# Attention with side work for the next four heads: 1.7 side steps per key block in place of 1.3

## The chip, the cores and the metric

The kernel runs on one core of one Trainium2 chip. The metric is the device time of one execution in microseconds; of the kernel before three executions are at hand, and their median is the time before. A profiled execution, recorded by the hardware, gives the trace from which all durations here are read.

## The reference

One inference step of a small decoder with two layers, for a prompt of 1024 tokens (16 learned meta tokens ahead of it) and for 8 samples of 4 new tokens that share the weights. The first layer is a causal convolution module and a feed-forward block with a convolution, the second is multi-head latent attention and the same kind of feed-forward block. The change is in the prompt's attention, which the reference computes so (cut; queries and keys are first normalised per head, and the last 32 values of a query are rotated by its position):

```python
def rms_norm(x, g):
    xf = x.astype(jnp.float32)
    y = xf * lax.rsqrt(jnp.mean(xf * xf, axis=-1, keepdims=True) + NORM_EPS)
    return (y * g.astype(jnp.float32)).astype(x.dtype)

def mla_queries(xn, pos, w_dq, q_lat_norm, w_uq, qnorm_nope, qnorm_rope):
    q = jnp.einsum('btl,lhd->bthd', rms_norm(xn @ w_dq, q_lat_norm), w_uq)
    q_nope = rms_norm(q[..., :QK_NOPE], qnorm_nope)
    q_rope = rope(rms_norm(q[..., QK_NOPE:], qnorm_rope), pos)
    return q_nope, q_rope
...
    k_nope = rms_norm(jnp.einsum('btc,chd->bthd', c, w_uk), knorm_nope)
    v = jnp.einsum('btc,chd->bthd', c, w_uv)
...
        s = (jnp.einsum('bqhd,bkhd->bhqk', qn_b, k_nope) +
             jnp.einsum('bqhr,bkr->bhqk', qr_b, kr)).astype(jnp.float32) * SM_SCALE
        s = jnp.where(kpos[None, :] <= qpos[:, None], s, NEG)
        p = jax.nn.softmax(s, axis=-1).astype(v.dtype)
        return jnp.einsum('bhqk,bkhd->bqhd', p, v)
```

There are 16 heads with 64 + 32 values per query and key and 64 values per output, in float32. The scores' precision is kept by splitting each operand into a high and a low part and multiplying three times (high by high, high by low, low by high).

## The kernel before, in words

The program goes through the phases one after the other: the first layer, then the prompt's attention (about 1415 to 1830 us in the profile), then the samples and the last feed-forward block. Only the attention's loop is touched.

**The loop.** One head after the other, n = 0 to 15. In head n, `values` takes the two halves of 512 queries: 5 key blocks for the first half and 9 for the second, so 14 blocks, counted x = 0 to 13. A block is three score matmuls of TensorE (L1347, L1349, L1350) into a PSUM tile p, the causal mask added on the diagonal by VectorE (L1352), the exponential by ScalarE into pf (L1354), and then the value matmul of the block before (L1337), so that TensorE has the scores of one block to do while the exponential of the last one runs. The width of a block is the number of queries that may see it: 512 for the early blocks, then 400, 272, 144 and 16 at the end of a half.

**What runs beside it.** At fixed x of head n the program calls steps for head n + 1: `query` (x = 0, transposes L1277 and splits into high and low, L135 to L138), `scores` (at the x in SAT; L1307, with the row maximum on VectorE, L1309 to L1314) and `shift` (x = SHAT = 12), which transposes the maxima (L1319, TensorE) and puts them as a further row into the query tile (L1323, VectorE). The first score matmul of head n + 1 needs L1323. `keys` comes at x = 8 to 10 of every second head, `metas` at x = 7 of every fourth; `finish` normalises a pair of heads on GpSimd's queue (L1380 on VectorE, L1384 on GpSimd).

**The side work.** Queries and keys are projected for four heads at a time, a group. At x = SIDE = 8 of heads 0, 4 and 8 a generator `side` is made for the next group. For groups 2 and 3 it has some 30 steps:
- `group_k`, 10 steps: the load of the weights; 5 steps of two blocks (matmuls L151, copy and square on ScalarE, sums L1160 on VectorE); the reciprocal root (`rsqrt`, L255 to L260, VectorE); three multiplies on GpSimd.
- `group_q`, 20 steps: the load; 9 projection steps, each six matmuls L151 of 384 columns, two copies L1193 and a square L1196 on ScalarE and the sums L1201 on VectorE; the reciprocal root, whose result is the tile rrq; then three pieces of three steps each: a multiply of q by rrq on GpSimd (L1209), a multiply on VectorE (L1215), and the rotation on VectorE (four multiplies L1103, then L1106 and L1107).

For group 1 the side work has 20 steps, since `group_q`'s projections are done before the loop: `group_k` and the scaling and rotary steps alone.

**Its pace.** At the end of every block the loop adds RATE (L46) to `due`, and takes one step of `side` for each whole 1 in it. What is left of `side` is run at x = 0 of the group's last head.

**What sets the final order.** The program is written in this order, and a scheduler then reorders each engine's queue by its own estimate of times and by the free buffers: score tiles p turn over in 3 PSUM buffers, which the projections use too, value tiles in 2, pf in 4.

Of the kernel before, what the change touches and what calls it, by code (L numbers as in the profile page):

```python
# [42 lines left out]
BLOCKS = ((0, 8), (8, 7), (15, 7))  # L43
WQ = 5
LAG = 3
RATE = 1.3  # L46
QAT = 0
AAT = (14, 34)
BAT = (12, 80)
# [69 lines left out]
class Prog:  # L119
# [989 lines left out]
    def attention(self, es):  # L1109
# [302 lines left out]
        def both(g):  # L1412
            yield from group_k(g)
            yield from group_q(g)
# [42 lines left out]
        for n in range(H):  # L1457
# [3 lines left out]
            for x, _ in enumerate(chain(values(n, 0), values(n, 1))):  # L1461
# [18 lines left out]
                if n % 4 == 0 and x == SIDE and n < H - 4:  # L1480
                    side = both(g + 1) if g else chain(group_k(1), nxt)
                due += RATE
                while due >= 1:
# [408 lines left out]
```

## Time and profile before

| | us |
|---|---|
| time, median of 3 executions | 2760.52 (2760.06 to 2764.99) |
| the profiled execution, its own time | 2764.3 |
| its span (first to last instruction) | 2762.4 |
| from head 0's L1319, just ahead of the attention loop, to head 15's | 1415.4 to 1801.4 |

The span is 1.9 us below the profiled execution's own time. TensorE's granted clock is 0.981 of full speed on the mean. In the views, a row has the busy time of an engine, or of a group of instructions (line, engine, operation, tile written from tiles read), with how many there were; a bracket at a row's end is the idle time of the engine ahead of it, and what ended that. PE is TensorE, PEld its weight loads, DVE VectorE, ACT ScalarE, POOL GpSimd, SP SyncE.

### The profile page before, as it was taken

To read this page: it belongs to the slowest core of one execution; us is meant where nothing else is said; L and a number is where in the kernel's file an instruction comes from. 1 tells how busy PE (TensorE), PEld (TensorE's weight loads), DVE (VectorE), ACT (ScalarE), POOL (GpSimd) and SP (SyncE) were. 2 spreads that over 40 slices of the span, in tenths; PEclk is the share of its full clock that TensorE was granted. 3 is DMA by queue.
4 is the path that set the end of the run, shared out by engine and by line. 5 is a ranking of instruction groups with operands and counts; after the bars stand their busy time and mean duration, and the time that the engine had idled before them with its cause. 6 is when DMAs were issued, how large, how long until landed. Compare 5 with 4: busy or idle time off the path is not lost.

```text
span 2762.4 us, 46569 instructions
## 1 busy us (share of the span) xinstructions
PE 2652.8 (96%) x16966; PEld 2448.0 (89%) x16966; DVE 1878.0 (68%) x3485; ACT 1356.2 (49%) x3701; POOL 711.0 (26%) x1019
## 2 busy tenths in 40 slices
PE   7999997999999999999889999999999999999999
PEld 6888876999999999999767776667999999999999
DVE  8899986578888875135677767676377777775232
ACT  6777775345444553023555555566245454453010
POOL 1567663024333330001111212110023333330000
PEclk9999997999999999999989999999999999999999
DMA  4211101502322236123100001267402222227122
GB/s 142 57 41 55 39 29 42 173 32 87 95 88 94 80 105 238 47 81 107 35 11 18 26 24 32 80 199 261 152 24 89 80 77 85 80 97 244 41 87 76
DMA packets 127769, 238.24 MB, mean 86 GB/s; under 512 B 39778, under 2 KB 81140, under 8 KB 127412
## 3 DMA queue, kind: packets, MB, share of 16 engines
q1 hardware_dynamic: 103828, 200.82, 22.6%
q0 software_dynamic: 9600, 32.36, 3.1%
q10 hardware_dynamic: 14112, 2.09, 0.5%
q8 instruction: 133, 2.18, 0.3%
q14 instruction: 96, 0.79, 0.1%
HBM read 183.90 MB, written 51.31 MB: 85 GB/s over the span
## 4 chain that ended last, share of the span: by engine, by line
PE 85%; DVE 6%; ACT 5%; DMA 2%; issue 2%; POOL 0%; SPq 0%; ACTq 0%; DVEq 0%; POOLq 0%
PE ps L796 30%; PE ps L175 22%; PE pk L654 5%; PE v L1337 5%; PE g L419 4%; PE ps L845 3%; PE p L151 2%; PE ps L197 2%; PE ps L1013 1%; PE po L1651 1%; PE p L1347 1%; PE p L1350 1%; PE p L1349 1%; PE s L1307 1%; PE sn L151 1%
## 5 line engine op out<-in xcount | busy, mean ns | idle before, releaser
L135 ACT ACTIVATE wh<-raw 128x512 fp32r<-128x512 f32 (+2 forms) x256 | 191.1, 749 | 542.0 <-PE ps L175 338.5
L136 DVE TENSOR_TENSOR wl<-raw,wh 128x512 fp32r<-128x512 f32 (+2 forms) x244 | 201.5, 829 | 111.4 <-ACT wh L135 109.2
L942 DVE TENSOR_TENSOR x<-ps,x 128x1074 f32<-128x1074 f32 (+1 forms) x48 | 61.0, 1270 | 293.1 <-PE ps L175 293.1
L766 DVE SCALAR_TENSOR_TENSOR c<-ub,c,c 128x1040 f32<-128x1040 f32 (+1 forms) x176 | 225.1, 1312 | 28.6 <-ACT c L763 27.6
L761 POOL COPY sb<-ub 128x32 f32<-128x32 f32 x88 | 88.8, 1011 | 400.9 <-DVE ub L807 363.2
L669 ACT ACTIVATE qq<-pk 128x64 f32<-128x64 f32 x736 | 158.1, 243 | 67.6 <-PE pk L654 67.5
L1337 PE MATMUL v<-pf,vf 128*128 128x512 f32 (+4 forms) x448 | 176.6, 478 | 10.0 <-ACT pf L1354 9.7
L663 POOL TENSOR_TENSOR sq<-sq 128x256 f32<-128x256 f32 (+4 forms) x229 | 140.2, 623 | 102.6 <-ACT sq L658 95.6
L175 PE MATMUL ps<-xh,wh 128*128 128x358 f32 (+1 forms) x672 | 148.3, 329 | 9.1 <-ACT xh L135 5.9
L1354 ACT ACTIVATE pf<-p 128x512 f32<-128x512 f32 (+4 forms) x224 | 99.0, 451 | 118.1 <-DVE p L1352 98.1
L669 ACT ACTIVATION_READ_ACCUMULATOR qq<-pk 128x1 f32 x736 | 153.9, 227 | 0.0
L523 DVE SCALAR_TENSOR_TENSOR a<-u,c,a 128x512 f32<-128x512 f32 x216 | 150.1, 745 | 4.9 <-ACT a L516 4.9
L175 PE MATMUL ps<-xh,wl 128*128 128x358 f32 (+1 forms) x672 | 147.6, 328 | 0.0
L175 PE MATMUL ps<-xl,wh 128*128 128x358 f32 (+1 forms) x672 | 147.4, 327 | 0.1
L175 PE MATMUL ps<-al,wh 128*128 128x358 f32 (+1 forms) x672 | 147.2, 327 | 0.0
L175 PE MATMUL ps<-ah,wl 128*128 128x358 f32 (+1 forms) x672 | 146.5, 326 | 0.0
L175 PE MATMUL ps<-ah,wh 128*128 128x358 f32 (+1 forms) x672 | 146.2, 326 | 0.0
L654 PE MATMUL pk<-ukh,ch 128*128 128x512 f32 x256 | 115.5, 452 | 25.6 <-ACT ch L135 13.4
L763 ACT ACTIVATE c<-ub,c 128x1074 f32<-128x1074 f32 (+1 forms) x88 | 101.3, 1185 | 59.7 <-DVE ub L807 46.8
L175 PEld LDWEIGHTS ps<-xh,wh 128*128 128x128 f32 x672 | 117.5, 191 | 12.7 <-ACT xh L135 6.8
L658 ACT ACTIVATE sq<-pk 128x512 f32<-128x512 f32 x164 | 99.8, 613 | 50.8 <-PE pk L654 48.5
L135 ACT ACTIVATE wh<-s 128x512 fp32r<-128x512 f32 x120 | 75.7, 631 | 94.9 <-PE ps L796 88.3
(599 smaller groups left out, 9100.4 us busy)
## 6 DMA issues: line engine op xcount, KB each, us to landing
raw<-wup SPq DMA_DIRECT2D x88, 512.0 KB, 3.5
pg<-ctn SPq DMA_DIRECT2D x128, 192.0 KB, 3.8
raw<-wdn SPq DMA_DIRECT2D x32, 448.0 KB, 3.3
raw<-pw SPq DMA_DIRECT2D x24, 512.0 KB, 3.9
d_a<-c POOLq DMA_DIRECT2D x22, 537.0 KB, 3.5
raw<-d_a SPq DMA_DIRECT2D x22, 537.0 KB, 5.2
d_a<-c POOLq DMA_DIRECT2D x22, 531.0 KB, 3.1
raw<-d_a SPq DMA_DIRECT2D x22, 531.0 KB, 5.3
```

The lines of the kernel that those rows point to most:

```text
L135: return (nc.scalar.activation(h, src, AF.Copy), (eng or nc.vector).tensor_tensor(out=l, in0=src, in1=h.bitcast(F32), op=ALU.subtract))
L136: (eng or nc.vector).tensor_tensor(out=l, in0=src, in1=h.bitcast(F32), op=ALU.subtract))
L175: nc.tensor.matmul(p[:, c, :ch], s[:, k * 128:(k + 1) * 128], m[k][:, off + c * ch:off + (c + 1) * ch], start=k == 0 and i == 0, stop=k == ...
L419: y = nc.tensor.matmul(p[:, 0], x[:, k * 128:(k + 1) * 128], m[k][:, t * ch:t * ch + ch], start=k == 0 and i == 0, stop=k == KD - 1 and i ...
L523: nc.vector.scalar_tensor_tensor(out=p[:, :ND] if j == n - 1 else acc, in0=x[:, j:j + ND], scalar=w[:, j:j + 1], in1=to if j == 1 else acc ...
L654: x = nc.tensor.matmul(ps, s[:, j, :], m[:, 512 * c:512 * c + 512], start=i == 0, stop=i == 2)
L663: nc.gpsimd.tensor_tensor(out=to, in0=v[:, :, :n], in1=v[:, :, n:2 * n], op=ALU.add)
L669: nc.scalar.activation(q, ps[:, 64 * h:64 * h + 64], AF.Square, accum_out=ss[:, p, 8 * c + h:8 * c + h + 1])
L763: x = nc.scalar.activation(c, ub, AF.Copy, scale=wd[:, t, 2:3])
L766: nc.vector.scalar_tensor_tensor(out=c[:, 2:pe], in0=ub[:, tap:tap + pe - 2], scalar=wd[:, t, tap:tap + 1], in1=c[:, 2:pe], op0=ALU.mult, ...
L796: nc.tensor.matmul(ps, w[:, s], m[:, lo:hi], start=first and k == 0 and i == 0, stop=k == KD // 2 - 1 and i == 2, skip_group_check=True)
L1337: nc.tensor.matmul(o[:, at_:], vf[:m, b, c], p[:m, :512 - at_], start=b == 0, stop=last)
```

## The change

The change is one number: the loop takes 1.7 side steps per block in place of 1.3.

```diff
-RATE = 1.3
+RATE = 1.7
```

The loop that uses it, which is as before:

```python
                due += RATE
                while due >= 1:
                    due -= 1
                    next(side, None)
```

For group 2 (made in head 4 at x = 8) the keys' steps end in head 4 rather than at the start of head 5; the nine projection steps of the queries come in head 5 at x = 0 to 5, before at x = 3 to 9; and the scaling and rotary steps at x = 6 to 11 of head 5, before from x = 10 of head 5 to x = 2 of head 6. Group 3 is the same in heads 8 to 10. For group 1 the scaling and rotary steps come in head 1 at x = 0 to 5, before at x = 2 to 9. No engine gets another instruction, and SyncE's queue is as before. The places that matter follow, in the order that the scheduler gives each engine.

**VectorE, where group 2's q is scaled and rotated.** rrq is the scale, q_... the q tile of group 2, scr scratch; L1352 masks a block's scores p. Before, in head 6:

```order
L1215 TENSOR_TENSOR scr<-q_18839,rrq 128x512
L1312 TENSOR_REDUCE m_19274<-s 128x1
L1309 ISA junk,m_19274<-s,mask 128x328
L1309 ISA m_19274 128x1
L1380 RECIPROCAL lq<-lq 128x16
L1103 TENSOR_TENSOR scr<-scr,tabqcos_16180 128x256
L1103 TENSOR_TENSOR scr<-scr,tabqsin_16186 128x256
L1103 TENSOR_TENSOR scr<-scr,tabqsin_16182 128x256
L1103 TENSOR_TENSOR scr<-scr,tabqcos_16184 128x256
L1352 TENSOR_TENSOR p<-p,trit 128x16
```

And now, at the end of head 5:

```order
L260 SCALAR_TENSOR_TENSOR rrq<-nr_t,nr_y 128x72
L1215 TENSOR_TENSOR scr<-q_18813,rrq 128x512
L1352 TENSOR_TENSOR p<-p,trit 128x128
L1103 TENSOR_TENSOR scr<-scr,tabqcos_16180 128x256
L1103 TENSOR_TENSOR scr<-scr,tabqsin_16186 128x256
L1103 TENSOR_TENSOR scr<-scr,tabqsin_16182 128x256
L1103 TENSOR_TENSOR scr<-scr,tabqcos_16184 128x256
L1106 TENSOR_TENSOR q_18813<-scr 128x8x2x16
L1352 TENSOR_TENSOR p<-p,trit 128x128
L1107 TENSOR_TENSOR q_18813<-scr 128x8x2x16
L1215 TENSOR_TENSOR scr<-q_18813,rrq 128x512
L1323 TENSOR_TENSOR qh<-p,pick 8x1024
```

The first piece's multiply and rotation moved from the middle of head 6 to the end of head 5: they now stand between the masks of that head's last wide blocks, and the second piece's multiply stands ahead of the shift L1323 of head 6.

**TensorE, the last blocks of head 5**, ahead of the shift's L1319. Matmuls with wq are the projections; qh, ql, k2h, k2l are the high and low parts of query and key. Before:

```order
L151 MATMUL p<-wq1h,qll_16157 64x384
L1347 MATMUL p<-qh,k2h_17072 128x400
L1349 MATMUL p<-qh,k2l_17073 128x400
L1350 MATMUL p<-ql,k2h_17072 128x400
L1337 MATMUL v<-pf,vf 128x512
L1347 MATMUL p<-qh,k2h_17072 128x272
L1349 MATMUL p<-qh,k2l_17073 128x272
L1350 MATMUL p<-ql,k2h_17072 128x272
L1347 MATMUL p<-qh,k2h_17072 128x144
L1349 MATMUL p<-qh,k2l_17073 128x144
L1350 MATMUL p<-ql,k2h_17072 128x144
L1337 MATMUL v<-pf,vf 128x400
```

Now:

```order
L1347 MATMUL p<-qh,k2h_17072 128x400
L1349 MATMUL p<-qh,k2l_17073 128x400
L1350 MATMUL p<-ql,k2h_17072 128x400
L1337 MATMUL v<-pf,vf 128x512
L1347 MATMUL p<-qh,k2h_17072 128x272
L1349 MATMUL p<-qh,k2l_17073 128x272
L1350 MATMUL p<-ql,k2h_17072 128x272
L1337 MATMUL v<-pf,vf 128x512
L1347 MATMUL p<-qh,k2h_17072 128x144
L1349 MATMUL p<-qh,k2l_17073 128x144
L1350 MATMUL p<-ql,k2h_17072 128x144
L1337 MATMUL v<-pf,vf 128x400
```

The last projection block has gone from here to earlier in the head, and a value matmul of 512 columns now stands between the scores of the 272- and the 144-column block.

**VectorE, from the shift of head 1 to the mask of that head's second block** (128x112), with the side steps of group 1. q_17192 is the q tile of group 1, ql the low part of the split query. Before:

```order
L1323 TENSOR_TENSOR qh<-p,pick 8x1024
L1160 TENSOR_REDUCE ssk<-scr 128x8
L1352 TENSOR_TENSOR p<-p,trit 16x16
L1160 TENSOR_REDUCE ssk<-scr 64x4
L1215 TENSOR_TENSOR scr<-q_17192,rrq 128x512
L138 SCALAR_TENSOR_TENSOR ql<-s,gain,qh 96x512
L1352 TENSOR_TENSOR p<-p,trit 128x112
```

Now:

```order
L1323 TENSOR_TENSOR qh<-p,pick 8x1024
L138 SCALAR_TENSOR_TENSOR ql<-s,gain,qh 96x512
L1103 TENSOR_TENSOR scr<-scr,tabqcos_16180 128x256
L1103 TENSOR_TENSOR scr<-scr,tabqsin_16186 128x256
L1103 TENSOR_TENSOR scr<-scr,tabqsin_16182 128x256
L1309 ISA junk,mx<-s,mask 128x144
L1309 ISA mx 128x1
L1103 TENSOR_TENSOR scr<-scr,tabqcos_16184 128x256
L138 SCALAR_TENSOR_TENSOR ql<-s,gain,qh 96x512
L256 TENSOR_SCALAR nr_y<-nr_v 128x36
L1106 TENSOR_TENSOR q_17192<-scr 128x8x2x16
L1352 TENSOR_TENSOR p<-p,trit 128x112
```

The keys' sums L1160 and the multiply L1215 moved ahead of L1323, and the four L1103 and one L1106, which came later, now stand between L1323 and the mask.

## The prediction

> **What bounds the kernel now.** I read the page first, then the busy time of each engine per head, then who TensorE waited for, then the timelines of DVE, POOL and PE where a head is longer than its like.
>
> ```profile
> span 2762.4 us, 46569 instructions
> PE 2652.8 (96%) x16966; PEld 2448.0 (89%) x16966; DVE 1878.0 (68%) x3485; ACT 1356.2 (49%) x3701; POOL 711.0 (26%) x1019
> ```
>
> TensorE is busy nearly throughout, so nothing gains unless it takes away time in which PE stands still or runs at half clock. The change only touches the attention loop, about 1415 to 1830 us. I cut that loop at the L1319 matmul, which comes once a head (x = 12), so that each window below is one head from shift to shift.
>
> ```profile
> 1444.10:1468.00 23.90, 22.76 (x105) 15.95 (x104) 20.25 (x77) 11.50 (x27) 5.16 (x6) 0.93 0.02 6
> 1468.00:1489.10 21.10, 20.33 (x102) 14.53 (x98) 14.38 (x47) 12.06 (x27) 6.22 (x8) 1.00 0.16 51
> 1539.60:1569.70 30.10, 29.55 (x154) 23.59 (x152) 21.02 (x88) 19.73 (x55) 5.23 (x7) 1.00 0.01 1
> 1569.70:1597.60 27.90, 24.09 (x103) 16.58 (x102) 23.73 (x79) 11.95 (x28) 11.54 (x12) 0.88 0.12 39
> 1678.20:1707.00 28.80, 23.97 (x103) 16.54 (x102) 25.62 (x78) 11.69 (x27) 12.13 (x14) 0.88 0.17 50
> ```
>
> Columns: length; busy PE, weight load, DVE, ACT, POOL; granted clock; DMA. The second row is a quiet head (head 1 to 2, no side work) with the same number of matmuls, 102 against 103, as the fourth and fifth rows: 21.10 against 27.90 and 28.80 us. These two are the ends of heads 5 and 9 and most of heads 6 and 10, where only the DVE and POOL steps of the side work are left. They lose 6.8 and 7.7 us. The first row, the same place of the first group, loses 2.8. Together 17.3 us: all that a better pace could win. The third row, where the projections run, is full (29.55 of 30.10): nothing to win there.
>
> Where the 6.8 us go, in head 6: DVE, then POOL, then PE.
>
> ```profile
> 1577.41 0.23 DVE L260 SCALAR_TENSOR_TENSOR rrq<-nr_t,nr_y 128x72 f32<-128x72 f32 x1
> ...
> 1579.32 1.13 DVE L1103 TENSOR_TENSOR scr<-scr,tabqcos 128x256 f32<-128x256 f32 x1
> 1580.38 2.87 DVE L1103 TENSOR_TENSOR scr<-scr,tabqsin 128x256 f32<-128x256 f32 x2
> ...
> 1583.51 0.17 DVE L1352 TENSOR_TENSOR p<-p,trit 128x16 f32<-128x16 f32 x1
> ```
> ```profile
> 1577.73 5.24 POOL L1209 TENSOR_TENSOR q<-q,rrq 128x1024 f32<-128x1024 f32 x3 [0.31 <-DVE mx L1314]
> ```
> ```profile
> 1583.95 0.61 PE L1337 MATMUL v<-pf,vf 128*128 128x16 f32 x2 [2.90 <-ACT pf L1354]
> ```
>
> As soon as the scale rrq is there, POOL multiplies three pieces of q (L1209) and DVE's rotary multiplies (L1103) stretch. The mask L1352 stands behind them in DVE's queue, the exponential waits for the mask, and PE waits 2.90 us. In head 10 the same collision, on another DVE instruction, and two PE gaps:
>
> ```profile
> 1685.84 4.75 DVE L1215 TENSOR_TENSOR scr<-q,rrq 128x512 f32<-128x512 f32 x1
> ```
> ```profile
> 1690.79 0.50 PE L1347 MATMUL p<-qh,kth 104*128 104x512 f32 x1 [2.42 <-DVE s L1292]
> ...
> 1693.41 0.61 PE L1337 MATMUL v<-pf,vf 128*128 128x16 f32 x2 [1.26 <-ACT pf L1354]
> ```
>
> The gap costs twice, since the clock falls behind it:
>
> ```profile
> 1446.38:1449.79 3.41, 2.60 (x13) 1.70 (x11) 3.41 (x11) 2.98 (x8) 0.57 (x2) 1.00 0.00 0
> 1449.79:1453.20 3.41, 3.41 (x10) 2.38 (x11) 3.41 (x13) 0.79 (x2) 0.11 (x1) 0.50 0.13 40
> ...
> 1579.50:1582.91 3.41, 1.54 (x7) 0.95 (x6) 3.41 (x3) 0.00 (x0) 3.41 (x3) 1.00 0.00 0
> 1582.91:1589.74 6.83, 5.79 (x12) 3.91 (x13) 5.94 (x20) 3.07 (x7) 1.82 (x5) 0.50 0.29 78
> ```
>
> After a stretch with PE busy 2.60 of 3.41 us the clock was 0.50 for 3.41 us; after 1.54 of 3.41, for 6.83 us with 5.79 busy, which is 2.9 us of work lost.
>
> **The change part by part.** No instruction is added or removed; SP's queue is unchanged. Side steps (about 30 in each of the groups 2 and 3, 20 in group 1) come sooner: the projections of group 2 in head 5 at x = 0 to 5 (before 3 to 9), its scaling and rotary steps at x = 6 to 11 of head 5 (before x = 10 of head 5 to x = 2 of head 6). On POOL, L1209 goes ahead of the clearing of the next q tile and of a DMA of the row sums; only the later normalisation L1384 waits for that, which PE never waits for. What counts is where rrq and L1103 stand among DVE's masks.
>
> Prices without the collision, from the first group, where POOL had been done:
>
> ```profile
> 1444.39 1.21 DVE L1323 TENSOR_TENSOR qh<-p,pick 8x1024 fp32r<-8x1024 f32 x1 [0.31 <-PE p L1319]
> ...
> 1446.54 0.67 DVE L1215 TENSOR_TENSOR scr<-q,rrq 128x512 f32<-128x512 f32 x1
> 1447.13 0.73 DVE L138 SCALAR_TENSOR_TENSOR ql<-s,gain,qh 96x512 fp32r<-96x512 f32 x1
> 1447.80 0.26 DVE L1352 TENSOR_TENSOR p<-p,trit 128x112 f32<-128x112 f32 x1
> ...
> 1448.95 0.40 DVE L1103 TENSOR_TENSOR scr<-scr,tabqcos 128x256 f32<-128x256 f32 x1
> ```
> ```profile
> 1567.43 1.02 PE L1337 MATMUL v<-pf,vf 128*128 128x512 f32 x2
> ...
> 1570.57 0.49 PE L1337 MATMUL v<-pf,vf 128*128 128x144 f32 x2
> 1571.24 0.50 PE L1347 MATMUL p<-qh,kth 104*128 104x512 f32 x1 [0.19 <-DVE qh L1323]
> ...
> 1574.90 1.12 PE L1337 MATMUL v<-pf,vf 128*128 128x512 f32 x2 [0.72 <-ACT pf L1354]
> ```
>
> *Group 2, end of head 5.* Call E the end of the 400-column block's score matmuls (1567.43 before). Its mask starts some 0.2 later, rrq follows, POOL starts at about E+0.7. Before, POOL's start to the mask behind the four L1103 took 1583.51 - 1577.73 = 5.78 us; the mask of the 144-column block now stands there, behind one L1106 (as L1103, about 0.35). So it runs at E+6.8, and mask to PE is 0.44 (1583.51 to 1583.95), somewhat more for 144 columns: PE's matmul at E+7.3. PE reached it 3.14 us after E before (1570.57 - 1567.43); one 512-column value matmul now stands between, which the projections used to follow, 0.85: ready at E+4.0. Stall 3.3. Next, L1107, L1215 and the shift L1323 start at about E+8.0, and 1.27 later (1569.97 to 1571.24 before, and as in group 1) the next head's first score matmul at E+9.25; PE is ready at E+7.7: 1.55 in place of 0.19. Then the first mask of head 6 lies behind four L1103 (1.35), two L138 (1.3), a maximum and L1106: E+12.4, its exponential 0.6, PE at E+13.3 where it would be ready at E+11.9: 1.4 in place of 0.72. Up to that point PE is 5.3 later than before. In return the gap of 2.90 and its half clock 2.9 go from the middle of head 6. But three gaps within ten us leave PE less busy than the 2.60 of 3.41 that sufficed at 1446, so half clock comes back: bounds 0 and 3.4 (one spell of 6.83 with PE full), and since PE partly waits in it, I take 2.4. Against the 6.8 - 0.3 lost before beyond those shared gaps this is about +1 us (bounds -2 and +3).
>
> *Group 3, head 9.* The same, one mask earlier: stalls of 3.0, 0.35, 0.5 and 1.4 = 5.25, plus 2.4 of clock = 7.65, against the 7.7 lost: 0 (bounds -3 and +2).
>
> *Group 1, head 0 to 1.* L1209 ran long before, no collision. But the shift L1323 now has a 64-row L1160 (half the time of the full one), L1215 (0.6) and a weight split (0.35) ahead of it, about 1 us late, and the first mask of head 1 lies behind L138, four L1103, a maximum, a second L138 and L1106: 4.45 after L1323 where it was 3.41 (1447.80 - 1444.39). Head 1 starts its value matmuls about 1.5 later, its third block 1.1 later, with one more stretch at half clock possible: +1.1 to +3, I take +2.
>
> *Packing.* Nine projections in fewer blocks hold the three score tiles in PSUM until ACT has read them: 0.5 over both groups, bounds 0 and 5 (below).
>
> Sum: +1 + 0 + 2 + 0.5 = +3.5 us. The profiled execution is 2764.3 us by its own time (span 2762.4 and 1.9 around it), 3.8 above the median 2760.5 of three runs that spread from 2760.06 to 2764.99; the terms are differences, so I add them to the median: **2764 us**, 0.13% slower. About 0.2%, 5.5 us, is what a measurement of this kernel can tell from no change, so this counts as none.
>
> **The clock, trace against rule.** The trace has a half-clock spell after gaps of at most 0.36 us (the stretch with 2.60 busy), and none behind the lone 0.72 us gap at 1574.9. The Trainium skill, "TensorE: Matmul & The Clock Gate", section "Why this matters for your kernels", says that throughput holds while gaps stay under about 3 us. By that rule the shorter gaps after the change would cost no clock and the sum would be lower by the clock terms; the spell at 1449.79 speaks against it.
>
> **The rivals.** (1) *The clock stays full* because the waits are split: possible, as the lone 0.72 us gap cost none; against it, three gaps come close together. The clock terms 2.4 + 2.4 and about 1.5 in group 1 fall away: 3.5 - 6.3 = -2.8, 2758 us, still no measurable change. This is the skill's rule as a rival. (2) *Slower: ACT becomes the bound of the packed projections* in heads 5 and 9.
>
> ```profile
> L1193 ACT ACTIVATE q<-p 128x192 f32<-128x192 f32 x32 | 10.6, 331 | 18.8 <-PE p L151 18.5
> L1196 ACT ACTIVATE scr<-p 128x384 f32<-128x384 f32 x32 | 15.8, 496 | 7.3 <-DVE scr L1103 4.4 <-DVE ssq L1201 2.7 <-DVE q L1107 0.2
> ```
>
> Each block costs ACT two copies and a square, 2 x 0.33 + 0.50 = 1.16; nine are 10.4 of its 19.73 us in the 30.10 window, the other 9.3 are 31% of it. Before, they lie in 7 steps of together 19.5 us (30.10 less seven quiet blocks of 21.10 / 14 = 1.51); in 6 steps PE needs 18.0, and ACT has 10.4 + 0.31 x 18.0 = 16.0 us of work in them. Where the exponentials are the widest it would be full, and from a full ACT on, PE waits for a score tile at each projection: some 0.25 us x 9 x 2 groups = 4.5, so 2769 us. (3) *Faster: the collision does not come back*, if DVE's L1103 get their turn between POOL's pieces. Then the first stalls of groups 2 and 3 (3.3 and 3.0) and their clock terms go: 3.5 - 11.1 = -7.6, 2753 us. Against it: both traces of before show DVE losing 2.9 to 4 us, and rrq, which starts POOL, stands directly ahead of L1215 and L1103. That the scheduler undoes the pace is ruled out by the order, which shows the moves.
>
> **How the numbers follow.** Forecast 0.48; rival 1 0.18; rival 2 0.22; rival 3 0.12. Of the forecast's own spread (2759 to 2769 by the bounds) I give about a quarter to more than 5.5 us slower. So slower 0.22 + 0.11 = 0.33, faster 0.12, same 0.55. The range for 8 in 10 takes in rivals 1 and 2 with their spread and part of rival 3: 2755 to 2773.
>
> **What would show it right or wrong.** Right: the windows of heads 6 and 10 near 21 to 23 us, the ones ahead of them, which now hold projections and rotary steps, longer by as much; a DVE L1103 or L1215 of over 1 us right behind each rrq of groups 2 and 3, with PE waiting about 3 us for the 144- or 272-column exponential of heads 5 and 9; PE waiting over 1 us for L1323 in head 6; half clock there. Rival 1: the same gaps at clock 1.00. Rival 2: PE gaps put down to scr or q copies. Rival 3: no long L1103. The prediction is wrong if the loop's length changes by over 5 us either way, or if the difference lies behind 1830 us, where the order of the next phase shifts a little too.

## The result, and the profile after

The changed kernel takes 2769.13 us (median of 16 executions, 2764.34 to 2775.61), the kernel before, in the same measurement, 2760.94 us (16 executions, 2757.38 to 2769.95). The ratio is 1.0028 with a 95% interval of 1.0019 to 1.0037: slower by 0.28%, 7.7 us. The forecast was 2764 and +3.5 us, "within 0.2%"; the time lies in the range, but just beyond that bound. The forecast counted its +3.5 us as no change; the interval leaves 1 out, so the kernel is slower. The profiled executions differ by as much: 2771.9 us with a span of 2770.1 now, 2764.3 with 2762.4 before.

From the page after, the span and the busy times:

```profile
span 2770.1 us, 46570 instructions
PE 2657.1 (96%) x16966; PEld 2450.0 (88%) x16966; DVE 1881.8 (68%) x3485; ACT 1357.0 (49%) x3701; POOL 707.7 (26%) x1019
```

The engines do the same work, so the 7.7 us are waiting and clock. The windows of after, the first five at the same places as the five of the prediction, then head 14 to 15 and the hand-over from the samples to the output projection (last L1651 to last L151):

```profile
1441.70:1465.60 23.90, 21.27 (x97) 14.53 (x96) 19.01 (x75) 9.84 (x23) 5.15 (x6) 1.00 0.02 6
1465.60:1486.80 21.20, 20.42 (x102) 14.62 (x100) 14.36 (x47) 12.03 (x27) 6.21 (x8) 1.00 0.16 51
1537.90:1568.60 30.70, 29.81 (x151) 23.21 (x150) 24.28 (x98) 19.28 (x53) 7.55 (x8) 1.00 0.01 1
1568.60:1597.70 29.10, 24.68 (x103) 17.77 (x102) 21.76 (x68) 12.24 (x27) 9.10 (x11) 0.82 0.11 37
1679.90:1707.90 28.00, 24.13 (x103) 16.77 (x102) 20.98 (x69) 12.30 (x28) 9.52 (x13) 0.88 0.20 67
1776.30:1807.60 31.30, 28.12 (x122) 20.59 (x121) 17.70 (x52) 16.93 (x38) 7.12 (x11) 0.84 0.68 212
1921.80:1956.60 34.80, 33.05 (x172) 32.32 (x171) 16.97 (x26) 15.94 (x29) 0.00 (x0) 0.80 0.69 243
```

The last two places before:

```profile
1775.40:1801.40 26.00, 23.79 (x123) 17.15 (x121) 17.28 (x52) 15.83 (x36) 3.55 (x6) 1.00 0.69 203
1919.30:1947.30 28.00, 27.21 (x172) 26.21 (x170) 15.58 (x25) 14.65 (x28) 0.00 (x0) 1.00 0.75 259
```

The windows of heads 6 and 10, forecast at 21 to 23 us, are at 29.10 (27.90 before) and 28.00 (28.80): that sign of being right did not come. Head 6's is at a granted clock of 0.82. And the hand-over, where no side step runs, takes 34.8 us in place of 28.0 at a clock of 0.80.

**In the loop** the collision came where the steps had it. Group 2 at the end of head 5, on POOL, DVE and PE:

```profile
1566.32 5.13 POOL L1209 TENSOR_TENSOR q<-q,rrq 128x1024 f32<-128x1024 f32 x3 [3.44 <-DVE rrq L260]
```
```profile
1566.20 0.69 DVE L1215 TENSOR_TENSOR scr<-q,rrq 128x512 f32<-128x512 f32 x1
1566.97 0.30 DVE L1352 TENSOR_TENSOR p<-p,trit 128x128 f32<-128x128 f32 x1
1567.18 1.76 DVE L1103 TENSOR_TENSOR scr<-scr,tabqcos 128x256 f32<-128x256 f32 x1
1568.86 2.87 DVE L1103 TENSOR_TENSOR scr<-scr,tabqsin 128x256 f32<-128x256 f32 x2
...
1572.33 0.29 DVE L1352 TENSOR_TENSOR p<-p,trit 128x128 f32<-128x128 f32 x1
```
```profile
1568.56 0.27 PE L1319 MATMUL p<-c,mx 128*8 128x128 f32 x1
...
1572.99 0.85 PE L1337 MATMUL v<-pf,vf 128*128 128x144 f32 x2 [3.63 <-ACT pf L1354]
...
1574.84 0.79 PE L1347 MATMUL p<-qh,kth 104*128 104x512 f32 x1 [0.79 <-DVE qh L1323]
```

POOL's multiplies and DVE's L1103 collide right behind rrq, the mask of the 144-column block stands behind them, and PE waits 3.63 us (forecast 3.3), then 0.79 for the shift (forecast 1.55). The third wait, forecast at 1.4, does not show. TensorE runs L1319, where the windows are cut, at 1568.56, ahead of the long wait, so the wait still falls into the window of head 6. Group 3 in head 9, PE:

```profile
1683.31 0.73 PE L1337 MATMUL v<-pf,vf 128*128 128x272 f32 x2 [3.10 <-ACT pf L1354]
1684.34 0.51 PE L1337 MATMUL v<-pf,vf 128*128 128x144 f32 x2 [0.24 <-ACT pf L1354]
```

3.10 and 0.24 against 3.0 and 0.35; of the other two waits, forecast at 0.5 and 1.4, one does not show and one is 0.46. The clock behind the gap of group 2:

```profile
1569.28:1572.69 3.41, 0.08 (x4) 0.00 (x0) 3.41 (x6) 0.04 (x1) 2.17 (x2) 0.97 0.00 0
1572.69:1576.10 3.41, 2.32 (x6) 1.62 (x6) 3.35 (x8) 1.57 (x4) 0.00 (x0) 0.50 0.00 0
1576.10:1579.50 3.40, 3.40 (x11) 2.68 (x11) 3.40 (x12) 2.35 (x6) 1.12 (x2) 0.50 0.00 0
1579.50:1582.90 3.40, 3.40 (x10) 2.32 (x11) 2.38 (x13) 0.82 (x2) 0.57 (x1) 0.53 0.03 4
```

Three stretches at half clock, not two: half of 2.32 + 3.40 + 3.40 is 4.6 us of lost work, where 2.4 was taken.

**Behind the loop** ScalarE's order had moved. ACT at the hand-over, before and then after (wh is the high half of the output projection's first weight, ob the last samples' result):

```profile
1917.27 1.04 ACT L135 ACTIVATE wh<-raw 128x1024 fp32r<-128x1024 f32 x1
1919.35 0.64 ACT L1662 ACTIVATE ob<-po,lr 64x128 f32<-64x128 f32 x2 [1.03 <-PE po L1651]
```
```profile
1921.92 0.64 ACT L1662 ACTIVATE ob<-po,lr 64x128 f32<-64x128 f32 x2 [1.03 <-PE po L1651]
...
1923.05 1.05 ACT L135 ACTIVATE wh<-raw 128x1024 fp32r<-128x1024 f32 x1
```

And PE after:

```profile
1922.34 0.55 PE L1663 MATMUL pp<-c,ob 64*128 64x64 f32 x2 [0.23 <-ACT ob L1662]
1924.15 0.66 PE L151 MATMUL ps<-xh,wh 128*128 128x354 f32 x1 [1.26 <-ACT wh L135]
```

Before, wh was ready ahead of ob and PE did not wait for it; now the scheduler puts wh behind ob and the first copy oth. PE waits 1.26 us, and the clock is at 0.50 for 13.7 us from 1924.04 on.

### The profile page after: what moved, and what is told of

It reads as the page before. It is cut to its first block, busy times and chain, and to the rows that moved or that the text cites. A ratio compares the mean times of both kernels' runs of the same rounds, so it can differ in the third digit from the quotient of the medians.

```text
span 2770.1 us, 46570 instructions
## 1 busy us (share of the span) xinstructions
PE 2657.1 (96%) x16966; PEld 2450.0 (88%) x16966; DVE 1881.8 (68%) x3485; ACT 1357.0 (49%) x3701; POOL 707.7 (26%) x1019
## 3 DMA queue, kind: packets, MB, share of 16 engines
q1 hardware_dynamic: 103828, 200.82, 22.2%
## 4 chain that ended last, share of the span: by engine, by line
PE 84%; DVE 7%; ACT 4%; DMA 2%; issue 2%; POOL 0%; SPq 0%; ACTq 0%; DVEq 0%; POOLq 0%
PE ps L796 30%; PE ps L175 22%; PE pk L654 5%; PE g L419 4%; PE v L1337 4%; PE ps L845 3%; PE ps L197 2%; PE p L151 2%; PE ps L1013 1%; PE p L1347 1%; PE p L1350 1%; PE p L1349 1%; PE po L1651 1%; PE s L1307 1%; PE ps L151 1%
## 5 line engine op out<-in xcount | busy, mean ns | idle before, releaser
L1337 PE MATMUL v<-pf,vf 128*128 128x512 f32 (+4 forms) x448 | 177.8, 481 | 14.8 <-ACT pf L1354 14.4
```

The lines of the kernel that those rows point to most:

```text
L1337: nc.tensor.matmul(o[:, at_:], vf[:m, b, c], p[:m, :512 - at_], start=b == 0, stop=last)
```

## The experiments

Theory A: the cost lies in the loop, by the prediction's steps. Theory B: it lies behind the loop, where the order changes as soon as anything ahead moves. Later expectations call them loop theory and tail theory. In this table every trace is cut at the starts of the same PE instructions: heads 0 to 13 from head 0's L1319 to head 14's, heads 14 and 15 to the last L1337, the hand-over from the last L1651 to the last L151. In the calm kernels the lines behind `group_q` are 7 higher (L1326 is L1319, L1284 is L1277).

| kernel | heads 0-13 | heads 14-15 | hand-over | ratio to before (95%) |
|---|---|---|---|---|
| before | 360.0 | 55.5 | 28.1 | 1 |
| after | 364.5 | 60.2 | 34.8 | 1.0028 (1.0019 to 1.0037) |
| g1_only | 360.2 | 55.8 | 28.1 | 1.0002 (0.9993 to 1.0012) |
| g2_only | 360.5 | 59.0 | 34.8 | 1.0031 (1.0022 to 1.0040) |
| g3_only | 360.1 | 56.8 | 29.5 | 1.0020 (1.0009 to 1.0031) |
| fast_no_mul | 356.1 | 55.8 | 34.7 | 1.0005 (0.9993 to 1.0017) |
| fast_wh_first | 365.8 | 58.5 | 28.5 | 1.0023 (1.0013 to 1.0032) |
| slow_wh_last | 360.1 | 55.9 | 34.8 | 1.0019 (1.0009 to 1.0029) |
| calm_1_3 | 354.3 | 55.5 | 28.7 | 0.9989 (0.9979 to 1.0000) |
| calm_1_7 | 355.0 | 59.1 | 29.2 | 1.0007 (0.9995 to 1.0019) |
| g2_wh_first | 362.4 | 55.1 | 31.8 | 1.0020 (1.0009 to 1.0030) |
| slow_no_mul | 350.1 | 55.6 | 28.1 | 0.9967 (0.9954 to 0.9980) |
| calm_1_4 | 350.3 | 55.2 | 31.2 | 0.9971 (0.9960 to 0.9983) |
| calm_1_6 | 350.1 | 58.2 | 28.7 | 0.9975 (0.9964 to 0.9986) |

**One group at a time: g1_only, g2_only, g3_only.** FAST is (0,), (1,) or (2,).

```diff
-RATE = 1.3
+RATE, FAST = (1.3, 1.7), (0,)
...
-        side, due = iter(()), 0.0
+        side, due = iter(()), [0.0, 0.0]
...
-                due += RATE
-                while due >= 1:
-                    due -= 1
+                due = [d % 1 + r for d, r in zip(due, RATE)]
+                fast = g in FAST
+                for _ in range(int(due[fast])):
                     next(side, None)
```

> The pace of 1.7 for group 1 alone (heads 0 to 3); all side work of groups 2 and 3 at 1.3 and at its old place. Theory A (the cost lies in the loop, where each group's scaling and rotary steps are): +1 to +2 us, about 2762.5 against 2761 before, in the windows of heads 0 and 1; nothing further back. Theory B (the cost lies behind the loop, where the scheduler orders the samples' matmuls otherwise as soon as anything ahead of them moves): +4 to +8 us, 2765 to 2769, as slow as the full change, with a longer spell of half clock between 1910 and 1960 us.

> The pace of 1.7 for group 2 alone (heads 4 to 6). Theory A: +2 us, about 2763, made of +0.7 in the window ahead of head 5's shift, +1.2 in the one behind it and +0.5 in head 4; a TensorE gap of about 3.6 us for the 144-column exponential. Theory B: +4 to +8 us, 2765 to 2769, whichever group is moved.

> The pace of 1.7 for group 3 alone (heads 8 to 10); its order behind the loop is that of the full change. Theory A: +1 us, about 2762. Theory B: +4 to +8 us, 2765 to 2769, and the trace shows the half clock between 1910 and 1960 us and ScalarE's wait for a page in head 14 as the full change does; then both belong to the order behind the loop. If they are absent there, they are chance.

Medians 2761.51, 2769.39 and 2764.82 us against 2760.35. Neither theory alone: g1_only is as A has it, g2_only and g3_only cost far more than their places in the loop. The order at the hand-over differs with them: wh is first in g1_only (28.1 us), late in the other two. g2_only has the long spell at half clock there (34.8), g3_only the same gap without it:

```profile
1918.30:1947.80 29.50, 27.33 (x173) 26.30 (x171) 14.62 (x25) 14.53 (x28) 0.00 (x0) 1.00 0.74 260
```

So the gap comes with the order, and the spell behind it, by g3_only's own expectation, in part by chance. That the hand-over makes g3_only slower by 0.20% is argued: its one trace has only 1.4 us more there.

**The hand-over alone: slow_wh_last, fast_wh_first, g2_wh_first.** One or two ordering edges between ScalarE instructions; the order of the loop stays.

The two wh_first kernels put the copies ob behind the first wh:

```diff
-                nc.scalar.activation(ob[:, e], po[e], AF.Copy, scale=lr[:, e:e + 1])
+                self.obs = [nc.scalar.activation(ob[:, e], po[e], AF.Copy, scale=lr[:, e:e + 1])] + (self.obs if e else [])
...
                 ws.append(self.weight(a["wo"][k], 1024))
+                for x in self.obs if k == 0 else ():
+                    self.follow(x, [self.last[0]])
```

slow_wh_last puts wh behind the first oth:

```diff
-                self.split(d(oth), d(otl), px[:, 64 * e:64 * e + 64].rearrange("p (h i) -> p h i", i=DS))
+                x = self.split(d(oth), d(otl), px[:, 64 * e:64 * e + 64].rearrange("p (h i) -> p h i", i=DS))
+                self.oth0 = self.oth0 if e else x[0]
...
                 ws.append(self.weight(a["wo"][k], 1024))
+                self.follow(self.last[0], [self.oth0])
```

> The kernel before (1.3 in all groups, loop unchanged) with the opposite edge: that weight split goes behind the first of the copies oth, as in the full change. Tail theory: a TensorE gap of about 1.3 us ahead of the projection's first matmul; +1.4 us without and +6.7 us with the spell of half clock, so 2762 to 2768. Loop theory: no change, 2760 to 2762.

The kernel before with nothing but this edge (PE's order is the same up to there) takes 2764.91 against 2759.44, ratio 1.0019 (1.0009 to 1.0029): the tail theory's 2762 to 2768. PE and the window:

```profile
1915.40 0.66 PE L151 MATMUL ps<-xh,wh 128*128 128x354 f32 x1 [1.26 <-ACT wh L135]
```
```profile
1913.10:1947.90 34.80, 33.14 (x172) 32.17 (x171) 16.52 (x25) 15.85 (x29) 0.00 (x0) 0.80 0.64 230
```

> The full change (1.7 in all groups) with one more ordering edge: the output projection's first weight split (wh, ScalarE) goes ahead of the last samples' copies ob, where the kernel before has it and the full change has it behind. The loop's order is that of the full change. Tail theory (most of the 7.7 us is that hand-over: TensorE waits 1.26 us for wh around 1922 us and then runs two spells at half clock): from the last L1651 to the last L151 the trace shows 28.1 us in place of 34.8, no spell of 13.7 us, and the time falls by 5 to 7 us to 2762 to 2764. Loop theory (the cost is that of the gaps in heads 5, 6, 9 and 10): the time stays at 2767 or more.

> Pace 1.7 in group 2 alone, as measured before at 8.6 us over the kernel before (ratio 1.0031), now with wh ahead of the copies ob. Tail theory (the hand-over from the samples to the output projection costs 1.4 us, or 6.7 with the spells at half clock): only the loop's 2.4 us are left, 2762 to 2764, ratio about 1.001, 28.1 to 28.7 us from the last L1651 to the last L151. Rival (the edge changes the trace there but the time is lost in the loop or in heads 14 and 15): 2766 to 2769, ratio 1.0025 or more.

Taking the wait away gave less than expected. The traces show 28.5 us in place of 34.8, as the tail theory has it, and 31.8 in place of 34.8, where it had 28.1 to 28.7: a spell of 6.8 us at half clock came there with wh first. But the times are 2767.24 (ratio 1.0023, the loop theory's side) and 2764.32 (1.0020, between the two). The gains against after and g2_only, 0.0005 and 0.0011 of the time or 1.4 and 3 us, are within the intervals of some 0.0010 each. fast_wh_first's own trace lost elsewhere: 365.8 us in heads 0 to 13 and 58.5 in heads 14 and 15. So slow_wh_last shows that the late wh costs time; what it costs in the full change is known only roughly, and taking it out there did not give a gain clear of the noise.

**The collision alone: fast_no_mul, slow_no_mul.** In `chunk`, c is 2 for group 0 and 4 for the others.

```diff
-                x = eng.tensor_tensor(out=w, in0=w, in1=s(0, 64), op=ALU.mult)
+                x = eng.tensor_tensor(out=w, in0=w, in1=s(0, 64), op=ALU.mult) if c == 2 else None
```

> The full change with GpSimd's multiplies of q by its scale (L1209, groups 1 to 3) left out, so that part of q stays unscaled; VectorE's order at the rotary steps stays as it is. Collision theory (VectorE's rotary multiplies stretch because GpSimd reads the same memory port): every L1103 takes 0.4 us, the gaps of 3.6 and about 3 us ahead of the 144- and 272-column exponentials go with their half clock, and the loop is 9 to 14 us shorter than the full change: 2756 to 2761. Rival (the masks wait for their place behind the four L1103 in VectorE's queue, whatever these take): gaps of over 1.5 us stay, the gain is under 4 us, 2765 or more.

> The kernel before (pace 1.3) with GpSimd's multiplies L1209 of the groups 1 to 3 left out, so that part of q stays unscaled; VectorE's order is that of before. Collision theory: the windows of heads 6 and 10 fall from 28.0 and 28.8 to 23 to 24 us, from head 0's shift to head 14's 350 to 352 in place of 360, and the time is 2749 to 2752. Rival (VectorE's own instructions delay the masks): windows of 26 us or more, 2757 or more.

DVE of fast_no_mul at the place where L1103 took 1.76 and 2.87 us:

```profile
1566.98 0.41 DVE L1103 TENSOR_TENSOR scr<-scr,tabqcos 128x256 f32<-128x256 f32 x1
1567.31 0.75 DVE L1103 TENSOR_TENSOR scr<-scr,tabqsin 128x256 f32<-128x256 f32 x2
```

The windows of heads 6 and 10, shift to shift, in fast_no_mul, then in slow_no_mul:

```profile
1568.37:1594.10 25.73, 23.99 (x103) 17.24 (x102) 18.29 (x65) 12.26 (x27) 6.26 (x8) 0.87 0.13 42
1676.29:1699.30 23.01, 21.36 (x104) 15.16 (x103) 17.04 (x63) 12.27 (x27) 7.76 (x11) 1.00 0.24 69
```
```profile
1569.64:1592.07 22.43, 21.50 (x103) 14.85 (x102) 21.59 (x77) 10.59 (x26) 6.34 (x9) 1.00 0.15 48
1673.86:1696.03 22.17, 21.03 (x104) 14.94 (x102) 21.27 (x77) 10.94 (x26) 7.16 (x10) 1.00 0.13 37
```

At 1.3 the multiplies cost 9.9 us of the loop (360.0 to 350.1) and as much of the time: 2749.65 against 2759.19. At 1.7 it is 8.4 us (364.5 to 356.1): the gap of 3.63 us is 0.16 there, but of the half clock in head 6, which the expectation had gone, 6.83 us stayed (0.87 in its window). The time there, 2762.93, misses the collision theory's range: that run had the hand-over's 34.7 us, which the expectation hadn't counted. Without any collision 1.7 is still 6 us longer in the loop than 1.3 (356.1 and 350.1). Of these, 1.2 lie in heads 0 and 1, 1.2 in heads 4 and 5, 1.6 in head 9 and the rest mainly behind head 6's shift. There PE waits 0.92 us for L1323 and 0.59 for the first exponential, which points to the place of the rotary steps; for the other parts the cause was not tried.

**No collision, with all the work: the four calm kernels.** All multiplies of a group first, and VectorE's scaling and rotation behind the last of them; wh first. calm_1_4 and calm_1_6 keep group 1 at 1.3.

```diff
-            for m, b0, nb in PIECES if g else ():
-                s = lambda i: rr[:m, i, 4 * b0:4 * b0 + 4 * nb].rearrange("p (a c b) -> p a c b", c=2, b=1)
-                yield from chunk(lambda lo, step, w: sub(q, m, b0, nb, lo, step, w), s, m, b0, nb, 4, nc.gpsimd)
+            todo = []
+            for m, b0, nb in PIECES if g else ():
+                s = lambda i, m=m, b0=b0, nb=nb: rr[:m, i, 4 * b0:4 * b0 + 4 * nb].rearrange("p (a c b) -> p a c b", c=2, b=1)
+                todo.append(chunk(lambda lo, step, w, m=m, b0=b0, nb=nb: sub(q, m, b0, nb, lo, step, w), s, m, b0, nb, 4, nc.gpsimd))
+                next(todo[-1])
+                yield
+            for x in todo:
+                yield from x
...
+                if c == 4:
+                    self.after(x, st["mul"])
```

> Pace 1.3, wh first; of each group 2 and 3 GpSimd's three multiplies L1209 come first, one a step, and VectorE's L1215 and L1103 wait for the last of them, so that the two engines don't read the same memory at the same time. Collision theory: no L1103 or L1215 over 0.8 us, the gaps of 2.90, 2.42 and 1.26 us and both spells of half clock in heads 6 and 10 go: 7 to 13 us less than before, 2748 to 2754. Queue theory (the masks suffer from the number of VectorE instructions among them, not from the collision): within 3 us of before, 2758 to 2764.

> The same at pace 1.7, wh first. Collision theory: gap of 3.6 us gone in heads 5 and 9, the loop at 356 us from head 0's shift to head 14's as without the multiplies (364.7 with the full change), 2752 to 2757, somewhat more than at 1.3 if the projections packed into fewer blocks cost ScalarE time. Queue theory: 2762 or more.

> Group 1 at 1.3, groups 2 and 3 at 1.4, wh first, GpSimd's three multiplies first and VectorE's scaling and rotation behind the last of them; these then lie behind head 6's shift and ahead of its keys. Collision theory: windows of heads 6 and 10 at 22 to 24 us and of heads 7 and 11 at 23.0, since the rotation no longer runs into the keys' splits as it did at 1.3: 351 to 353 us from shift 0 to shift 14, 2751 to 2753. Queue theory: 2757 or more.

> The same with groups 2 and 3 at 1.6. Collision theory: as at 1.4, but some 1 to 1.5 us more in heads 5 and 9, where the projections are packed into fewer blocks: 352 to 355 us from shift 0 to shift 14, 2752 to 2755. Queue theory: 2757 or more.

calm_1_3, 2757.74 against 2759.44, gained less than the collision theory had and lies at the edge of the queue theory's 2758 to 2764, though its loop is 5.7 us shorter in the trace. The rotation, now later, ran into the keys' splits of head 6, and PE waited there in turn:

```profile
1592.94 0.27 PE L1326 MATMUL p<-c,mx 128*8 128x128 f32 x1 [1.01 <-DVE k2l L136]
...
1595.36 0.61 PE L1284 MATMUL s<-c,q 128*96 128x128 f32 x4 [1.16 <-DVE k2l L136]
```

At 1.4 it lies behind the shift and ahead of the keys. POOL and DVE of calm_1_4:

```profile
1568.41 4.33 POOL L1209 TENSOR_TENSOR q<-q,rrq 128x1024 f32<-128x1024 f32 x3 [3.47 <-DVE rrq L260]
```
```profile
1573.34 0.69 DVE L1215 TENSOR_TENSOR scr<-q,rrq 128x512 f32<-128x512 f32 x1
1574.30 0.42 DVE L1103 TENSOR_TENSOR scr<-scr,tabqcos 128x256 f32<-128x256 f32 x1
1574.63 0.75 DVE L1103 TENSOR_TENSOR scr<-scr,tabqsin 128x256 f32<-128x256 f32 x2
```

and its heads 6 and 10:

```profile
1568.01:1590.27 22.26, 21.34 (x103) 14.98 (x102) 19.60 (x69) 11.76 (x27) 10.47 (x11) 1.00 0.12 38
1671.89:1694.10 22.21, 21.33 (x103) 14.99 (x102) 18.59 (x68) 10.93 (x26) 11.90 (x14) 1.00 0.26 80
```

No long instruction, no half clock, 22.3 and 22.2 us where the kernel before had 27.9 and 28.8. calm_1_4 takes 2750.97 us against 2759.19, ratio 0.9971 (0.9960 to 0.9983): it beats both kernels, and calm_1_6 (2753.40) does too. Pace, order and wh differ from the kernel before at once; slow_no_mul, with nothing but the multiplies left out, gained as much. calm_1_7, with group 1 at 1.7 too, keeps 355.0 us in the loop and gains nothing in time (2762.93): its trace fits the collision theory, its time the queue theory's 2762 or more, with 59.1 us in heads 14 and 15.

## Where the prediction was right and where it was short

- *Group 1, +2 forecast.* The traces that ran it at 1.7 with no other change to these heads (after, the kernels g1_only, fast_no_mul, fast_wh_first and calm_1_7) take 53.7 us on the mean from head 0's shift to head 2's, the nine others 52.0: +1.7. Right in size, in part by luck: the forecast's 2 holds about 1.5 for half clock, but four of these five traces have none there, and in after PE's waits in head 1 make the loss, 2.5 us where they were 1.1. In g1_only the mask of head 1 comes 1451.64 - 1447.20 = 4.44 after L1323, as forecast (4.45):

```profile
1447.20 1.21 DVE L1323 TENSOR_TENSOR qh<-p,pick 8x1024 fp32r<-8x1024 f32 x1
...
1451.64 0.26 DVE L1352 TENSOR_TENSOR p<-p,trit 128x112 f32<-128x112 f32 x1
```

- *Group 2, +1 forecast (-2 to +3).* From head 4's shift to head 7's: 87.9 us on the mean of the four traces with it at 1.7 and the multiplies at their old place, 85.2 in the four at 1.3: +2.6. Behind the long gap two terms were mis-sized and nearly cancel, which is luck: the waits were 3.63, 0.79 and none, where 3.3, 1.55 and 1.4 stood, and the clock cost 4.6, where "since PE partly waits in it, I take 2.4" stood; together 9.0 for 8.65. The clock's part varies: fast_wh_first, with the same order, was at half clock there for 6.8 us, after, g2_only and g2_wh_first for 10.2. Another 1.2 us are lost ahead of head 6's shift (next but one).
- *Group 3, 0 forecast (-3 to +2).* 87.6 against 86.4 us: +1.2, of which 1.6 lie in head 9 and are partly given back in head 10. There the waits were shorter than forecast and the clock cost more: PE was busy for 6.37 us at half clock from 1685.10 on, 3.2 lost for the 2.4 taken.
- *Packing, +0.5 forecast.* It is within the groups' sums, and was put too low: from head 4's shift to head 6's the time goes from 57.6 to 58.8 us with 311 matmuls in both, and in head 9 from 30.15 to 31.78. fast_no_mul has the same 58.8 and 31.78, so this is not the collision; whether the packed projections or the masks at the end of the head cost it was not tried. ScalarE did not become the bound (19.28 of 30.70 us in head 5, no PE wait for scr or a copy of q), so rival 2 fell, though its 2769 us is the time that came.
- *Rival 1*, no half clock, fell: 0.50 over three stretches behind the 3.63 us gap. *Rival 3*, no collision, fell: L1103 took 1.76 and 2.87 us.
- *The sum* of the loop, by these means, is 1.7 + 2.6 + 1.2 = 5.5 us where 3.5 stood; 4.5 in the two profiled executions. With heads 14 and 15, which the prediction counts to the loop, these two differ by 9.2. The prediction called itself wrong if the loop changes by over 5 us: it was, by the 5.5 and by the 9.2, and only the 4.5 stays below.
- *What failed* is the step that ended the list of what moves: the prediction saw that "the order of the next phase shifts a little too" and gave it no term. One ScalarE instruction that changed sides at the hand-over costs there, over the traces, (34.8 + 34.8 + 29.5 + 34.7 + 34.8) / 5 = 33.7 us against 29.2 on the mean of the nine with wh first: +4.6. By its other test, a difference that lies behind 1830 us, it was wrong as well.

5.5 + 4.6 is 10.1, at the upper end of the measured 5.2 to 10.2. In the two profiled executions the stages differ by -3.6 us up to head 0's shift, +4.5 in heads 0 to 13, +4.7 in heads 14 and 15, -3.0 up to the hand-over, +6.7 in it and -1.6 behind: 7.7 in sum, since three stages are shorter by 8.2 together. So the split of the 7.7 us is not settled: the stage from the start to head 0's shift, whose order is the same everywhere, took 1409.8 to 1416.4 us in these traces, as much as what is to be told apart.

Heads 14 and 15 took 60.2 us after and 55.5 before, with the same order there on PE, DVE and ACT in all 14 traces. The difference is half clock: eight traces have none there and take 55.1 to 55.9 us, one has 3.4 us of it (56.8), four have 6.8 (58.2 to 59.1), and after has 10.2, in two spells:

```profile
1787.50:1794.33 6.83, 6.83 (x22) 5.75 (x21) 4.67 (x15) 3.90 (x8) 0.94 (x2) 0.50 0.97 314
1804.57:1807.98 3.41, 3.41 (x13) 2.25 (x13) 1.02 (x2) 2.95 (x8) 1.39 (x4) 0.50 1.01 343
```

What brings it on is open. In the profiled execution of after ScalarE waited longer for the samples' first page there, and the exponentials stand behind that wait (before, then after):

```profile
1783.29 0.63 ACT L135 ACTIVATE ch<-pg 128x512 fp32r<-128x512 f32 x1 [1.45 <-DMA pg<-ctn]
```
```profile
1785.60 0.63 ACT L135 ACTIVATE ch<-pg 128x512 fp32r<-128x512 f32 x1 [2.89 <-DMA pg<-ctn]
```

A wait of over 2 us there came in three traces, each with half clock, but three others have half clock without it. So it may be chance; whether the pace plays a part was not tried.

## What to carry to other kernels

A scheduler that reorders whole queues carries a local change far: compare the orders to the end of the program, and price each place where an instruction that another engine waits for has changed sides, however far from the edit. Side work that is moved should be judged by what its engines do to each other at the new place: GpSimd and VectorE slowed each other here at 1.3 and at 1.7 until one waited for the other. What that was worth hung on the pace: ratios to the kernel before of 0.9989 at 1.3, 0.9971 at 1.4 and 1.0007 at 1.7, with wh first in all three. Where a gap brings half clock, price it by that, not by its own length.

## What the runs showed of the hardware

- *A short gap can cost several times its length.* The 1.26 us wait for wh (with 0.23 ahead of it) was followed by 13.7 us at half clock in four of five traces. The spells begin on a fixed grid of 3.41 us (in after from head 5 on at 1572.46, 1685.10, 1787.50, 1804.57 and 1924.04 us, which are 33, 30, 5 and 35 steps apart), but the busy share of the stretch ahead does not decide alone: after 2.03 us busy of 3.42 half clock came, in g3_only after 1.89 of 3.41 it did not (the two stretches, of after and of g3_only):

```profile
1920.62:1924.04 3.42, 2.03 (x15) 1.34 (x13) 1.51 (x2) 2.03 (x6) 0.00 (x0) 1.00 0.68 208
```
```profile
1919.71:1923.12 3.41, 1.89 (x11) 1.73 (x12) 2.80 (x5) 2.84 (x4) 0.00 (x0) 1.00 0.53 180
```

  The Trainium skill, "TensorE: Matmul & The Clock Gate", section "Why this matters for your kernels", asks for no idle gaps of over about 3 us between matmul bursts if throughput is not to drop. These traces show drops behind a gap of 1.26 us. Nor is the late wh needed for one: calm_1_4, with the order of the kernel before at the hand-over, was at half clock for 6.83 us there, behind a stretch with 2.61 us busy of 3.40.
- *GpSimd and VectorE on the same memory.* GpSimd's three multiplies took 4.33 us alone and 5.13 beside VectorE; VectorE's L1103 0.41 alone and 1.76 beside GpSimd, the next two together 2.87. The same pair stood in the way just ahead of head 15 in fast_wh_first, where the normalisation L1384 stretched a split and with it delayed the shift (POOL, DVE and PE):

```profile
1800.27 2.35 POOL L1384 TENSOR_TENSOR o<-o,lb 128x1024 f32<-128x1024 f32 x1 [7.19 <-DMA lb<-d_l]
```
```profile
1800.70 2.47 DVE L136 TENSOR_TENSOR wl<-tm,wh 32x512 fp32r<-32x512 f32 x1 [2.82 <-ACT wh L135]
```
```profile
1804.56 0.50 PE L1347 MATMUL p<-qh,kth 128*128 128x512 f32 x1 [2.01 <-DVE qh L1323]
```

  The Trainium skill, "SBUF — State Buffer", section "Who interferes with whom", calls the ports that the two share an exclusive lock; these rows agree: the split, 0.68 us in the trace before, starts 0.43 us behind the multiply's start and ends 0.55 behind its end.
